# Attention of a hybrid diffusion step in units of 512 queries: plain float32 value products on two column halves

## The chip, the core and the metric

The kernel runs on one core of one Trainium2 chip. Its engines work side by side, each through its own queue in order: TensorE (PE, with its weight loads PEld), VectorE (DVE), ScalarE (ACT), GpSimd (POOL) and SyncE (SP, which issues DMAs). The metric is the device time of one execution in microseconds (us). The runs of the kernel before took 2245.47 to 2252.65 us, with a median of 2249.08 over three.

## The reference

One layer with 128 context tokens and 1024 latent tokens, all in float32. Its input projection feeds multi-head attention (8 heads) and an mLSTM; both are projected, gated and merged, and a feed-forward part follows. The part that the change touches is the attention of one block of queries:

```python
def block(args):
    qn_b, qp_b = args
    s = jnp.einsum('bqhd,bkhd->bhqk', qn_b, k_nope) + jnp.einsum('bqhr,bkr->bhqk', qp_b, k_pe)
    p = jax.nn.softmax(s.astype(jnp.float32) * MLA_SCALE, axis=-1)
    return jnp.einsum('bhqk,bkhv->bqhv', p.astype(v.dtype), v)
```

A query has 64 + 32 = 96 features per head, a value 64. Latent queries read 1024 latent and 128 cached context keys, which is 9 blocks of 128 keys; the 128 queries of the new context read only their own 128 keys.

## The kernel before

Most products are made exact by splitting: an operand x becomes hi (x rounded to float32r, `R32`) and lo (the rest), by `hi` on ACT (L69) and `lo` on DVE (L75). `mm3` (L98 to L100) then adds three float32r products hi*hi, hi*lo, lo*hi. Products of plain float32 (`F32`) operands are one instruction in the program, which leaves two records in the trace.

`attention` goes through the heads. For each head the 1024 latent queries are cut into four units of 256, and there is a small unit (`None`) for the 128 context queries. A unit's work, in program order:

- `maxima`: for each 128 queries three products of the leading parts against 384 keys (tile `mx`), a maximum on DVE for each (`sm`, then `mr`), and one product per 128 queries with a selector `sel` that turns the maxima into a row of the queries' operand. This is done for the unit ahead while the present one is scored.
- `scores`: five slots of two key blocks; each slot has two `mm3` into one bank `st`, the exponential on ACT (`p`), its split into `ph` and `pl` (DVE, in two slots of five POOL), and the running sum `es` on POOL.
- `values`: with a lag of two slots, four products of 256 columns per slot into `pv`. The stationary tile `v` holds 64 columns of hi and 64 of lo.
- `output`: the sum of `es` over its partitions by one-column products with `ones`, a reciprocal `rd` split into `rh` and `rl`, four diagonal matrices `dr` on ACT, two products that broadcast them, then a copy, an addition and a multiplication (`av`), a split (`ao`) and a store to `d_att`.

Beside this runs `o_mlstm`, the projection of the mLSTM's branch (tiles `hm` and `mm`, 384 columns): a share of its pieces is emitted in every slot. At the end `first` emits products of the attention's own projection (288 columns, tile `att`), which don't need the last heads' outputs; the tiles of the last pair of heads are reloaded from `d_att` by POOL's queue (`aload`).

The order in each engine's queue is not the program order: a scheduler in the build (`schedule_with_timeline_sim=True`) places ready instructions of later steps ahead. The queues then run in that fixed order.

Of the kernel before, what the change touches and what calls it, by code (L numbers as in the profile page):

```python
# [19 lines left out]
P = 128  # L20
# [36 lines left out]
class K:  # L57
# [25 lines left out]
    def load_w(self, src, kt, w, bufs=None):  # L83
        """Stream one weight block [P, kt, w] from DRAM and split it exactly."""
# [10 lines left out]
    def mm3(self, out, lhs, rhs, first, last):  # L95
        """out += lhs.T @ rhs for operands split in two parts."""
        mm = self.nc.tensor.matmul
        mm(out, lhs[0], rhs[0], start=first, stop=False)  # L98
        mm(out, lhs[0], rhs[1], start=False, stop=False)  # L99
        self.pe = mm(out, lhs[1], rhs[0], start=False, stop=last).ins  # L100
# [11 lines left out]
    def rsqrt(self, ssq, width, n, pool):  # L112
        """1/sqrt(ssq/n + eps) on the vector engine: exponent estimate and three Newton steps."""
# [12 lines left out]
    def row_rstd(self, rbc, acc, n, pool, pp, tag, chunks=CHUNKS, more=None):  # L126
        """rbc[:, t] = 1/sqrt(sum_p (acc[p, t] + more[p, t])/n + eps) on every partition."""
# [30 lines left out]
    def modulate(self, raw, t, sc, sh, k):  # L158
        """raw = t * sc + sh with the context's and the sample's own columns."""
# [4 lines left out]
    # ------------------------------------------------------------------  # L164
# [74 lines left out]
    def tick(self, n=1):  # L239
        """Emit n pieces of the work that runs beside the products."""  # L240
# [18 lines left out]
    def rows(self, rbc, acc, n, pool, pp, tag):  # L259
        """rbc[:, t] = 1/sqrt(sum_p acc[p, t]/n + eps) on every partition."""  # L260
# [28 lines left out]
    def inputs(self):  # L289
        """Everything that reads the modulated input (all of w_in), the mLSTM and the attention's projections."""  # L290
# [38 lines left out]
    def start(self, vp):  # L329
        """Norm and modulation of the input, and the mLSTM's values."""  # L330
# [44 lines left out]
        def row(f):  # L375
            """Shift (f even) or scale of block 6 + f // 2 of the features, as rows against the broadcast condition."""
# [166 lines left out]
    def t_ops(self, X, xp):  # L543
        """The four sums on the moving side."""
# [29 lines left out]
    def z_lat(self, x):  # L574
        """Latents and their norms, and the tile with gates and rotary key."""
# [40 lines left out]
    def z_qk(self, h, x):  # L616
        """q and k of one mLSTM head, S^T and k^T."""
# [29 lines left out]
    def z_big(self, p, x):  # L647
        """sigmoid(zmo) * g_mlstm for tiles 0-7, the sigmoids of the branch gates after them."""
# [17 lines left out]
    def background(self):  # L666
        """Columns of the modulation that are used after the mixer, as rows against the broadcast condition."""
# [41 lines left out]
    def krope(self):  # L709
        """Rotary keys, 288 tokens to a row."""  # L710
# [85 lines left out]
        # N = -M, A = log of the denominator's floor  # L796
# [24 lines left out]
    def lat_kv(self):  # L821
        """The key and value latent, back from DRAM and split."""
# [19 lines left out]
    def stage(self):  # L842
        """Half a slot for a projected block."""
# [11 lines left out]
    def proj(self):  # L855
        """Keys, values and queries of the attention from the latents."""
# [94 lines left out]
    def fill(self, n=1):  # L951
        """Emit n column chunks of the attention's projections."""
# [5 lines left out]
    # ------------------------------------------------------------------  # L958
    FILL = (17, 1, 1, 0, 1)

    def z2(self, mm):
# [4 lines left out]
        self.ready = False  # L966
        head = None
# [71 lines left out]
    def mfront(self, d, c, carried, second, S, E, Q, W):  # L1039
        """Operands of one chunk of one direction, four heads."""  # L1040
# [20 lines left out]
    def mback(self, d, c, carried, second, A, Q, K, C, mp, pp, side, load):  # L1061
        """Products, state update and output of the chunk."""
# [46 lines left out]
    def mpost(self, c, out, ssq, sgs, mp, pp):  # L1109
        """Norm, output gate and transposition of a finished chunk."""  # L1110
# [22 lines left out]
    # ------------------------------------------------------------------  # L1133
    def operands(self, pool):
        """Queries, keys and values of one head in two parts; row 96 adds -max of a query to its scores."""
        q = pool.tile([QK + 1, 2, T], R32, name=self.nm("q"))
        k = pool.tile([QK + 1, 2, NK], R32, name=self.nm("k"))
        v = pool.tile([P, NCH + 1, P], R32, name=self.nm("v"))
# [4 lines left out]
    def head_load(self, h, pool=None):  # L1143
        """Queries, keys (context, latent, cache) and values of one head, as column blocks."""
        G = self.nc.sync
        v = self.wp.tile([P, NCH + 1, AV], F32, name=self.nm("rv"), tag="wr", bufs=self.wb[0])
# [18 lines left out]
        G.dma_start(v, self.d_vo[h])  # L1165
        return q, k, v

    def head_split(self, h, raw):
        q, k, v = self.sets[h % 2]
        rq, rk, rv = raw  # L1170
# [5 lines left out]
        self.hi(v[:, :, 0:AV], rv)  # L1176
        self.lo(v[:, :, AV:], rv, v[:, :, 0:AV])
        yield 1

    SLOTS = 5  # L1180
    LAG = 2

    def attention(self):
# [6 lines left out]
        with tc.tile_pool(name="at", bufs=1, reuse_waits="tile") as ap:  # L1190
            self.ap, self.pp = ap, pp
            first = lambda shape, tag, bufs, dt=R32: ap.tile(shape, dt, name=self.nm(tag), tag=tag, bufs=bufs)
            for tag in ("ph", "pl"):
                first([P, 2, 256], tag, 4)
            first([P, 2, 256], "es", 2, F32)
            first([P, 2, 2, P], "dr", 1)
            first([AV, 256], "av", 2, F32)
            first([AV, 2, 256], "ao", 2)
            self.sets.append(self.operands(ap))
            self.onr = ap.tile([P, AV], R32, name="onr")  # L1200
            self.hi(self.onr, self.ones[:, 0:AV])
            self.sel = ap.tile([P, 3 * P], R32, name="selr")
            for i, x in enumerate((0.0, 1.0, 0.0)):
                self.hi(self.sel[:, i * P:(i + 1) * P], self.ident, x)
# [847 lines left out]
```

## Time and profile before

| | |
|---|---|
| runs, us | 2249.08, 2252.65, 2245.47 |
| profiled execution | span 2242.8 us from the first to the last instruction; its time with what lies around the span is not recorded |
| granted TensorE clock, mean | 0.966 |
| attention, first maxima to last division | 848 to 1263 us |

The profile shows one execution. Busy shares are of the span. A matmul's record reaches from its start to its modelled end, and records overlap, so the work of TensorE is better read from the distance between two starts. "Idle before" names what ended an engine's wait. The granted clock is the share of full speed that TensorE was given.

### The profile page before, as it was taken

The page shows a single profiled execution, that of the slowest core. Times are in us where ns is not written, and L with a number is a line of the kernel's source. Part 1 is how long each engine was busy: PE and PEld are TensorE (multiplying, and loading weights), DVE is VectorE, ACT ScalarE, POOL GpSimd, SP SyncE. Part 2 cuts the span into 40 slices and gives each one's busy share as a digit, 9 for nine tenths or more (in the row PEclk, how much of TensorE's full clock was granted, in tenths as well). Part 3 has the DMA queues.
Part 4 walks back from the last instruction along what each step waited for, and adds up shares of the span by engine and source line. Part 5 has one row for each costly group of instructions (what it writes and reads, how often), then busy time and mean ns, then how long its engine had stood idle before and what let it go on. Part 6 is the DMA issues. An engine that isn't in the chain of part 4 may idle for free.

```text
span 2242.8 us, 40186 instructions
## 1 busy us (share of the span) xinstructions
PE 2083.1 (93%) x14713; PEld 1998.2 (89%) x14713; DVE 1659.5 (74%) x2998; ACT 1068.0 (48%) x2225; POOL 1127.2 (50%) x850
## 2 busy tenths in 40 slices
PE   6799999999989987999999999879999999989898
PEld 2799998999978776998998999879999999989897
DVE  6725745988845879998987666899755565799895
ACT  4322333445445556777776435444322222356464
POOL 3612122667624415877877543677867634431411
PEclk8899999999999998999999999999999999999899
DMA  7121244555479775322224575223555522557664
GB/s 286 63 93 59 90 142 124 164 174 183 152 241 330 238 230 175 90 74 65 84 66 102 170 224 157 86 83 122 186 177 183 175 89 80 161 173 248 206 201 138
DMA packets 234532, 340.97 MB, mean 152 GB/s; under 512 B 18110, under 2 KB 170398, under 8 KB 233310
## 3 DMA queue, kind: packets, MB, share of 16 engines
q1 hardware_dynamic: 225790, 328.73, 46.0%
q0 software_dynamic: 4848, 6.06, 1.1%
q10 hardware_dynamic: 3696, 3.61, 0.5%
q8 instruction: 116, 1.90, 0.4%
q14 instruction: 82, 0.67, 0.1%
HBM read 250.55 MB, written 87.80 MB: 151 GB/s over the span
## 4 chain that ended last, share of the span: by engine, by line
PE 42%; DVE 16%; DMA 7%; POOL 6%; issue 6%; ACT 2%; SPq 1%; DVEq 0%; POOLq 0%; ACTq 0%
PE mm L98 10%; PE mm L100 10%; PE mm L99 10%; DVE wo L75 4%; DMA pr<-w_fo 3%; DVE sm L1374 2%; DVE pl L75 1%; PE st L98 1%; PE pv L1437 1%; PE pv L1438 1%; PE st L100 1%; PE st L99 1%; PE mx L1372 1%; DMA N<-d_nm 1%; PE p L1079 1%
## 5 line engine op out<-in xcount | busy, mean ns | idle before, releaser
L100 PE MATMUL mm<-th,wo 128*128 128x288 f32 x1840 | 546.8, 298 | 14.0 <-DVE wo L75 13.7
L98 PE MATMUL mm<-th,wo 128*128 128x288 f32 x1840 | 547.6, 298 | 2.7 <-DVE zo L1658 1.1
L99 PE MATMUL mm<-tl,wo 128*128 128x288 f32 x1840 | 546.2, 297 | 0.0
L100 PEld LDWEIGHTS mm<-th,wo 128*128 128x128 f32 x1840 | 348.9, 190 | 18.2 <-DVE wo L75 17.6
L75 DVE TENSOR_TENSOR wo<-wr,wo 128x512 fp32r<-128x512 f32 (+1 forms) x317 | 314.6, 1008 | 59.4 <-ACT wo L69 54.4
L98 PEld LDWEIGHTS mm<-th,wo 128*128 128x128 f32 x1840 | 348.2, 189 | 4.5 <-issue 1.6
L99 PEld LDWEIGHTS mm<-tl,wo 128*128 128x128 f32 x1840 | 348.3, 189 | 0.1
L69 ACT ACTIVATE wo<-wr 128x512 fp32r<-128x512 f32 (+1 forms) x317 | 187.5, 607 | 147.9 <-PE mm L100 69.5
L69 ACT ACTIVATE wo<-ws 128x512 fp32r<-128x512 f32 x188 | 116.7, 627 | 271.7 <-PE mm L100 160.5
L75 DVE TENSOR_TENSOR wo<-ws,wo 128x512 fp32r<-128x512 f32 x188 | 186.7, 996 | 62.1 <-ACT wo L69 61.9
L100 PE MATMUL mm<-xh,wo 128*128 128x288 f32 x616 | 184.7, 301 | 10.3 <-DVE wo L75 10.3
L1642 POOL TENSOR_TENSOR ws<-wr,ws 128x512 f32<-128x512 f32 x47 | 62.3, 1326 | 243.5 <-DVE wo L75 238.2
L99 PE MATMUL mm<-xl,wo 128*128 128x288 f32 x616 | 184.7, 300 | 0.0
L98 PE MATMUL mm<-xh,wo 128*128 128x288 f32 x616 | 184.2, 299 | 0.5 <-ACT wo L69 0.5
L1420 POOL TENSOR_TENSOR es<-es,p 128x512 f32<-128x512 f32 (+1 forms) x96 | 129.4, 1348 | 34.8 <-ACT p L1403 19.9
L98 PE MATMUL mm<-B,wo 128*128 128x288 f32 x456 | 134.8, 296 | 2.6 <-DVE zo L1658 1.7
L100 PE MATMUL mm<-B,wo 128*128 128x288 f32 x456 | 134.8, 296 | 0.0
L99 PE MATMUL mm<-B,wo 128*128 128x288 f32 x456 | 134.8, 296 | 0.0
L701 POOL TENSOR_TENSOR wm<-wm,sr 128x512 f32<-128x512 f32 x64 | 100.1, 1567 | 65.2 <-DVE mj L700 49.2
L100 PEld LDWEIGHTS mm<-xh,wo 128*128 128x128 f32 x616 | 118.1, 192 | 12.7 <-DVE wo L75 12.5
L98 PEld LDWEIGHTS mm<-xh,wo 128*128 128x128 f32 x616 | 118.2, 192 | 0.7 <-ACT wo L69 0.7
L99 PEld LDWEIGHTS mm<-xl,wo 128*128 128x128 f32 x616 | 118.4, 192 | 0.0
(443 smaller groups left out, 6076.6 us busy)
## 6 DMA issues: line engine op xcount, KB each, us to landing
wr<-w_ff SPq DMA_DIRECT2D x56, 512.0 KB
wm<-wm SPq DMA_DIRECT2D x32, 512.0 KB
wr<-d_w SPq DMA_DIRECT2D x32, 512.0 KB
d_z<-zo SPq DMA_DIRECT2D x48, 288.0 KB
d_g<-uu SPq DMA_DIRECT2D x44, 288.0 KB
wr<-w_big SPq DMA_DIRECT2D x24, 512.0 KB
wr<-w_fo SPq DMA_DIRECT2D x24, 512.0 KB
pr<-w_fo SPq DMA_DIRECT2D x40, 256.0 KB
```

Of the source, the lines that this page charges most:

```text
L69: i = self.nc.scalar.activation(out, in_, AF.Copy)
L75: return self.nc.vector.tensor_sub(out, in_, f32v(hi)).ins
L98: mm(out, lhs[0], rhs[0], start=first, stop=False)
L99: mm(out, lhs[0], rhs[1], start=False, stop=False)
L100: self.pe = mm(out, lhs[1], rhs[0], start=False, stop=last).ins
L701: nc.gpsimd.tensor_tensor(w[:, n], w[:, n], sr[:, 1], op=ALU.mult)
L1079: self.pe = mm(p1, A[:, h], V[:, h], start=True, stop=not carried).ins
L1372: nc.tensor.matmul(s[:, :kc], q[0:QK, 0, q0 + t * P:q0 + (t + 1) * P], k[0:QK, 0, k0 + j * kc:k0 + (j + 1) * kc], start=True, stop=True)
L1374: nc.vector.tensor_reduce(sm[:, 3 * t + j:3 * t + j + 1], s[:, :kc], axis=AX.X, op=ALU.max, negate=True)
L1420: G.tensor_tensor(U["sum"][:, :m], U["sum"][:, :m], p[:, :m], op=ALU.add)
L1437: nc.tensor.matmul(pv[:, :n], v[:, i], ph[:, e, :n], start=c + e == 0, stop=False)
L1642: G.tensor_tensor(s4, a12, s2, op=ALU.subtract)
```

## The change

- A unit has 512 queries (`QN`), so a head has two latent units and the small one. A slot of `scores` is one key block with 512 queries, nine slots to a unit.
- The exponentials `p` stay plain float32 and are not split; neither are the values, whose tile `v` has 64 columns and is filled by a DMA after the splits of the next head's queries and keys.
- `values` waits until a batch of a unit's blocks is ready (blocks 0 to 3, then 4 to 8) and emits plain float32 products of 64 stationary columns: even blocks into partitions 0 to 63 of `pv`, odd ones into 64 to 127, and the ninth block with half of its queries in each.
- `output` broadcasts the sum with two products of `ones` (64 columns) on the two halves, takes the reciprocal of 256 columns, adds the two halves and multiplies. The diagonal matrices and the selector are gone.
- `maxima` of all units are one stream, which runs up to two units ahead; the row of 512 maxima is written by four products of 128 columns with the identity.
- `o_mlstm` is spread over 136 - 11 slots in place of 168 - 13, so it ends earlier relative to the units.

```diff
-            units = [(h, b) for h in range(HA) for b in ((0, 1, 2, 3, None) if h < HA - 1 else (None, 0, 1, 2, 3))]
+            units = [(h, b) for h in range(HA) for b in ((0, None, 1) if h < HA - 1 else (None, 0, 1))]
...
-            NS, N0, NOM = HA * (4 * self.SLOTS + 1), 13, 88
+            NS, N0, NOM = HA * (2 * NCH - 1), 11, 88
...
-        p = self.wp.tile([P, 2, 256], F32, name=self.nm("p"), tag="ws", bufs=3)
-        self.ia = nc.scalar.activation(p[:, :m, :n], st[:, :m, :n], AF.Exp).ins
-        ph, pl = (ap.tile([P, 2, 256], R32, name=self.nm(x), tag=x, bufs=4) for x in ("ph", "pl"))
-        self.hi(ph[:, :m, :n], p[:, :m, :n])
...
+        self.mm3(st[:, :n], (k[:, 0, ks], k[:, 1, ks]), (q[:, 0, qs], q[:, 1, qs]), True, True)
+        p = U["P"][c] = ap.tile([P, self.QN], F32, name=self.nm("p"), tag="p", bufs=self.PBUF)
+        self.ia = nc.scalar.activation(p[:, :n], st[:, :n], AF.Exp).ins
...
-            nc.tensor.matmul(pv[:, :n], v[:, i], ph[:, e, :n], start=c + e == 0, stop=False)
-            self.pe = nc.tensor.matmul(pv[:, :n], v[:, i], pl[:, e, :n], start=False, stop=i == kb[-1]).ins
...
+            if len(todo) > 1:
+                parts = [(todo.pop(0), 0, n) for _ in range(2)]
+            else:
+                c = todo.pop(0)
+                parts = [(c, t * n // 2, n // 2) for t in range(2)]
+            for g, (c, q0, w) in enumerate(parts):
+                self.pe = nc.tensor.matmul(pv[g * AV:(g + 1) * AV, q0:q0 + w], v[:, kb[c]], U["P"][c][:, q0:q0 + w], start=c < 2,
+                                           stop=c == U["nc"] - 1, skip_group_check=True).ins
...
-        for t in range(nt):
-            nc.tensor.matmul(pv[:, 256 + t:257 + t], U["sum"][:, 0, t * P:(t + 1) * P], self.ones[:, 0:1], start=True, stop=True)
...
+        bc = self.bank(self.pp, "pv")
+        for g in range(2):
+            nc.tensor.matmul(bc[g * AV:(g + 1) * AV, :m], self.ones[:, 0:AV], U["sum"][:, g * m:(g + 1) * m], start=True, stop=True,
+                             skip_group_check=True)
```

TensorE's queue amid the latent units of one head. `pv` is the accumulator, `st` the scores, `mx` the maxima, `mm` the mLSTM's projection; the shape is that of the output. Before, the value products of two slots stand together, four to a slot:

```order
L1372 MATMUL mx_12035<-k_6950,q_6949 128x384
L1437 MATMUL pv_11792<-ph_11726,v_9240 128x256
L1438 MATMUL pv_11792<-pl_11727,v_9240 128x256
L1437 MATMUL pv_11792<-ph_11726,v_9240 128x256
L1438 MATMUL pv_11792<-pl_11727,v_9240 128x256
L1437 MATMUL pv_11792<-ph_11751,v_9240 128x256
L1438 MATMUL pv_11792<-pl_11752,v_9240 128x256
L98 MATMUL mm_11684<-hm_9497,wh_11191 128x384
```

All of them use the full 128 columns, like their neighbours. In the changed kernel, within one unit:

```order
L100 MATMUL mm_10610<-hm_9430,wl_10340 128x384
L1439 MATMUL pv_10690<-p_10623,v_9235 64x512
L1373 MATMUL mx_10630<-k_9234,q_9233 128x384
L1373 MATMUL mx_10646<-k_9234,q_9233 128x384
L98 MATMUL st_10677<-q_9233,k_9234 128x512
L99 MATMUL st_10677<-q_9233,k_9234 128x512
L100 MATMUL st_10677<-q_9233,k_9234 128x512
L1439 MATMUL pv_10690<-p_10643,v_9235 64x512
L1439 MATMUL pv_10690<-p_10662,v_9235 64x512
L98 MATMUL st_10697<-q_9233,k_9234 128x512
```

The scheduler has taken the batch apart: a 64-column product of one half stands alone between 128-column products, and a pair follows later.

At the unit's end, after the change, the ninth block and the broadcast of the sum stand together behind one product of 512 columns:

```order
L100 MATMUL st_10774<-q_9233,k_9234 128x128
L1439 MATMUL pv_10690<-p_10755,v_9235 64x512
L1439 MATMUL pv_10690<-p_10770,v_9235 64x256 x2
L1452 MATMUL pv_10794<-es_10625,ones 64x256 x2
L98 MATMUL mm_10742<-hm_9309,wh_10738 128x384
```

Before, the one-column products of the sum (L1449) and the two broadcasts (L1462) stood apart, with other products between them.

Behind the last division of the stage the queue before goes on with the mLSTM's projection, 110 products ahead of the first that reads the reloaded tile; its beginning:

```order
L1462 MATMUL pv_14795<-dr_14881,onr 64x256
L98 MATMUL pv_15028<-att_14408,wo_14965 128x288
L99 MATMUL pv_15028<-att_14408,wo_14965 128x288
L98 MATMUL mm_14929<-hm_9308,wh_14720 128x384
L99 MATMUL mm_14929<-hm_9308,wh_14720 128x384
```

Those 24 products of 384 columns are gone from this place. After, 45 products of 288 columns stand there; the last of them and the first reader of the reloaded tile (`att_12761`):

```order
L98 MATMUL st_12861<-rq_2349_12574,wo_12854 128x288
L99 MATMUL st_12861<-rq_2349_12574,wo_12854 128x288
L100 MATMUL st_12861<-rq_2349_12574,wo_12854 128x288
L98 MATMUL mx_12678<-att_12761,wo_12644 128x288
L99 MATMUL mx_12678<-att_12761,wo_12644 128x288
```

So the reader stands 45 rows behind the last division, where 110 stood before.

More of the change, by code (lines that the diff above doesn't have):

```diff
@@ L1192, in attention @@
             first = lambda shape, tag, bufs, dt=R32: ap.tile(shape, dt, name=self.nm(tag), tag=tag, bufs=bufs)
[L1193 to L1198, printed above, removed]
-            self.sets.append(self.operands(ap))
[L1200 to L1204, printed above, removed]
+            first([P, self.QN], "p", self.PBUF, F32)
+            first([P, self.QN], "es", 2, F32)
+            first([P, self.QN // 2], "av", 2, F32)
+            first([P, 2, self.QN // 2], "ao", 2)
+            self.sets.append(self.operands(ap))
+            self.idr = ap.tile([P, P], R32, name="idr")
+            self.hi(self.idr, self.ident)
             for tag in ("mm", "pv", "st", "mx"):
@@ L1210, in attention, with ahead @@
             side = []
-            units = [(h, b) for h in range(HA) for b in ((0, 1, 2, 3, None) if h < HA - 1 else (None, 0, 1, 2, 3))]
-            for _ in self.maxima(*units[0]):
-                pass
+            units = [(h, b) for h in range(HA) for b in ((0, None, 1) if h < HA - 1 else (None, 0, 1))]
+            mx = [self.maxima(*u) for u in units]
+            at = 0
+            def ahead(i, n=1):
+                nonlocal at
+                while n and at <= min(i, len(units) - 1) and units[at][0] in self.split:
+                    if next(mx[at], None) is None:
+                        at += 1
+                    else:
+                        n -= 1
@@ L1255, in attention @@
                                 next(self.om, None)
[L1256 to L1259 removed]
+            while late:
+                self.values(late)
             self.ps = {}
@@ L1427, in values, with ripe @@
+    def ripe(self, late, n):
+        U = late[0][1]
+        last = U["batch"][0][-1]
+        return any(t <= n and u is U and c == last for t, u, c in late)
+    def values(self, late):
+        nc = self.nc
+        U = late[0][1]
+        b = U["batch"].pop(0)
+        del late[:len(b)]
         h, n, kb = U["h"], U["n"], U["kb"]
         v = self.sets[h % 2][2]
-        if c == 0:
+        if b[0] == 0:
             while len(self.post) > 1:
```

182 lines of the change are left out of this document (81 added, 101 removed).

## The prediction

> **What bounds the kernel now.** I read the page's busy shares first, then the windows around attention, then the groups of instructions there, the waits, and single rows of the timeline.
>
> ```profile
> PE 2083.1 (93%) x14713; PEld 1998.2 (89%) x14713; DVE 1659.5 (74%) x2998; ACT 1068.0 (48%) x2225; POOL 1127.2 (50%) x850
> ```
>
> TensorE is busy 93% of the span, so time spent on it anywhere reaches the end. All edited lines run in the attention stage, from the first maxima at 848 us to the last division at 1263 us:
>
> ```profile
> core 0: us, PE busy (x) PEld busy (x) DVE busy (x) ACT busy (x) POOL busy (x), PEclk, DMA share, GB/s
> 848.00:900.00 52.00, 40.27 (x218) 34.11 (x217) 49.33 (x79) 36.16 (x72) 34.11 (x25) 0.80 0.53 161
> 900.00:1250.00 350.00, 331.83 (x2284) 314.57 (x2283) 307.16 (x611) 251.19 (x578) 262.92 (x212) 0.97 0.29 80
> 1250.00:1263.00 13.00, 12.28 (x86) 12.01 (x85) 5.42 (x9) 3.66 (x11) 5.38 (x6) 1.00 0.28 79
> ```
>
> The columns are length, then busy time of PE, weight loads, DVE, ACT, POOL, then granted clock. The first 52 us are bound by DVE (49.3 busy) and run at a clock of 0.80. After that PE is busy 95% and DVE 88%: two engines near their limit.
>
> PE's busy times overlap, so its work must be counted by distances between starts:
>
> ```profile
> 1060.49 0.28 PE L98 MATMUL st<-q,k 97*128 97x256 f32 x1
> ...
> 1061.91 0.28 PE L1382 MATMUL mx<-selr,mr 128*1 128x256 f32 x1
> 1062.21 0.22 PE L1462 MATMUL pv<-dr,onr 128*64 128x128 f32 x1
> 1062.27 0.39 PE L1372 MATMUL mx<-k,q 96*128 96x384 f32 x1
> 1255.07 0.34 PE L98 MATMUL mm<-hm,wh 128*128 128x384 f32 x1
> ...
> 1255.60 0.33 PE L98 MATMUL mm<-hm,wh 128*128 128x384 f32 x1
> 30.70 0.56 PE L267 MATMUL mm<-ones,ar 128*128 128x1 f32 x4
> 31.18 3.60 PE L356 MATMUL mx<-wm,silc 128*2 128x512 f32 x8
> 34.71 0.27 PE L267 MATMUL mm<-ones,ar 128*128 128x1 f32 x1
> 28.58 1.02 PE L356 MATMUL mx<-wm,silc 128*2 128x512 f32 x2
> 29.53 0.38 PE L280 MATMUL mm<-dg,ones 128*128 128x128 f32 x1
> 1500.62 0.40 PE L100 MATMUL mm<-th,wo 128*128 128x288 f32 x1 [1.08 <-DVE wo L75]
> 1500.86 0.30 PE L98 MATMUL mm<-th,wo 128*128 128x288 f32 x1
> ```
>
> In split (fp32r) products, 256 columns take 0.118 us (twelve products from 1060.49 to 1061.91), 128 take 0.06 and 384 take 0.177. The plain float32 product L356 leaves two records per product; eight last 3.60 with the last 0.59 of it, so (3.60 - 0.59)/7 = 0.430 a record and 0.86 for 512 columns. Half a record is 0.215, the stream of 512 columns, so a split product of 512 takes 0.215 + 0.0105 = 0.2255 (the 0.0105 is what 0.118 holds beyond 0.1075). A float32 product of one column has records at about 0.10 (0.56 less the 0.27 of one, over three). The 288-column products of the tail stand 0.133 apart.
>
> **The change part by part**, in us of PE time.
>
> ```profile
> L98 PE MATMUL st<-q,k 97*128 97x256 f32 x288 | 86.1, 299 | 1.5 <-ACT p L1403 0.9 <-ACT q L1383 0.4
> L1437 PE MATMUL pv<-ph,v 128*128 128x256 f32 x288 | 81.8, 299 | 5.7 <-DVE av L1467 5.7
> L1372 PE MATMUL mx<-k,q 96*128 96x384 f32 x192 | 65.2, 375 | 10.6 <-DVE sm L1374 9.8
> L1382 PE MATMUL mx<-selr,mr 128*1 128x256 f32 x72 | 20.0, 289 | 8.3 <-DVE mr L1377 4.0 <-DVE mr L1379 3.7 <-DVE sm L1374 0.4
> L1462 PE MATMUL pv<-dr,onr 128*64 128x256 f32 x64 | 17.7, 284 | 0.1
> L1449 PE MATMUL pv<-ones,es 128*128 128x1 f32 x128 | 16.3, 230 | 0.3 <-POOL es L1422 0.3
> ```
>
> Scores: 3 x 288 products of 256 columns (102.0) become 432 of 512 (97.4): -4.6. The maxima stay at 192 products. Their row transposes go from 72 x 0.118 to 72 of 128 columns at 0.06: -3.9 with rounding to 0.064.
>
> Values and division before: 576 x 0.118 = 68.0, the context's 16 at 0.06 = 1.0, 144 one-column records x 0.10 = 14.4, broadcasts 64 x 0.118 + 16 x 0.06 = 8.5; together 91.9. After, end to end: 128 products of 512 columns x 0.86 = 110.1, 64 of 256 x 0.43 = 27.5, 32 of 64 columns at about 0.12 = 3.8; together 141.5. Two halves can overlap only where products of different halves stand next to each other in PE's queue. In the built order the 224 products stand in 134 separate runs, 78 of them one single product of 512 columns; there are 90 neighbours of different halves. A product's two records use the same half, so each pair of neighbours overlaps by one record: 21 x 0.43 + 49 x 0.215 + 20 small = 20.6. Net 141.5 - 20.6 - 91.9 = +29.0. Whether halves overlap at all no row shows; the bounds are none (+49.6) and full halving to 70.8 (-21.1). I take the overlap only where partners stand, as in the order.
>
> Going between 64-column and 128-column products: L356 has two stationary columns, its neighbours 128. L267 starts at 34.71, which is 8 x 0.430 + 0.09 after 31.18; L280 at 29.53, where 28.58 + 0.86 gives 29.44: again 0.09. The first product behind also lasts longer since its weights could not be loaded ahead; the restart at 1500.62 shows that price, 0.40 against 0.30. For 64 columns I take half of it:
>
> ```profile
> L1462 PEld LDWEIGHTS pv<-dr,onr 128*64 128x64 f32 x80 | 11.0, 138 | 2.2 <-ACT dr L1459 1.2 <-issue 0.2
> L356 PEld LDWEIGHTS mx<-wm,silc 128*2 128x2 f32 x48 | 4.3, 95 | 31.4 <-issue 19.1 <-ACT silc L393 6.4 <-DMA wm<-wm 5.9
> ```
>
> since 62 more columns cost 0.138 - 0.095 = 0.043. One run then costs 0.09 + 0.05 going in and 0.09 + 0.10 coming out, 0.33; 134 runs cost +44.2. Bounds: 0 if the 0.09 belongs to L356 alone and the loads hide, 51 if both loads are full ones.
>
> A rule speaks against the change here. L356's weight load is hidden, for its records follow at the bare stream of 0.430. The Trainium skill, TensorE: Matmul & The Clock Gate, Part 3 (The mechanism), says that a weight load overlaps running products only when the row group differs; column halves share their rows. By it each of the 448 records would show its load of 0.05, an estimate of +22 on the sum; the 0.430 of the same tile speaks against it, and I take nothing.
>
> What the other engines shed:
>
> ```profile
> L75 DVE TENSOR_TENSOR pl<-p,ph 128x512 fp32r<-128x512 f32 x96 | 88.5, 924 | 20.9 <-ACT ph L69 18.7 <-issue 1.9
> L75 DVE TENSOR_TENSOR rl<-rd,rh 128x2 f32<-128x2 f32 x32 | 22.1, 691 | 0.3
> L1374 DVE TENSOR_REDUCE sm<-mx 128x1 f32<-128x384 f32 x192 | 99.7, 543 | 9.9 <-PE mx L1372 9.3
> L69 ACT ACTIVATE ph<-p 128x512 fp32r<-128x512 f32 x128 | 79.0, 626 | 3.5 <-PE pv L1437 1.3 <-PE pv L1438 1.0
> L1466 DVE TENSOR_TENSOR av<-av,pv 64x256 f32<-64x256 f32 x31 | 12.5, 402 | 0.2 <-ACT av L1465 0.2
> L1451 DVE RECIPROCAL rd<-pv 128x2 f32<-128x2 f32 x32 | 5.0, 157 | 3.8 <-PE pv L1449 3.8
> ```
>
> DVE loses 110 of 362 us (pl and rl) and gains 16 reciprocals over 256 columns, without a row: between 0.4 each (an addition over 256) and 20 (0.157 for two columns, times 128). A reciprocal that slow would show at each unit's end; I take about 0.5, 8 in all, since the other elementwise rows of 256 lie there. ACT loses 79 and more. POOL keeps 128 sums and loses 64 subtractions. None of them is near its limit any more, so these gains count only through PE's lost time.
>
> That lost time: PE's counted work is 341 (102.0 + 91.9 + 8.5, scores of the context 1.4, maxima 33.9, 552 products hm x 0.174 = 96, 51 tail products x 0.133 = 6.8) in 415 us, so 74 are lost: 30.6 idle by the windows, 52 x 0.20 + 350 x 0.03 = 21 by the clock, the rest restarts. Nearly all named waits are DVE's:
>
> ```profile
> PE mx L1372 <- DVE sm L1374: 10.0, 13, 2.0
> PE pv L1437 <- DVE av L1467: 5.7, 5, 2.5
> PE mx L1382 <- DVE mr L1377: 4.0, 6, 1.0
> ```
>
> I take 40 of the 74 as saved; bounds 0 and 60. The early stage keeps its splits of hm and the maxima on DVE and now needs twelve maxima before the first score.
>
> The end: the last division is covered less.
>
> ```profile
> 1262.74 0.28 PE L1462 MATMUL pv<-dr,onr 128*64 128x256 f32 x1
> 1265.25 0.52 SPq L1472 DMA_DIRECT2D d_att<-ao  x1
> 1270.54 1.45 POOL L1312 DMA_DIRECT2D att<-d_att  x2
> att<-d_att POOLq DMA_DIRECT2D x14, 288.0 KB, 6.6
> ```
>
> From the last division to the landing of the reload are 1270.54 + 6.6 - 1262.74 = 14.4. Before, 110 products (24 hm, 86 of 288) stand behind it ahead of the first use: 24 x 0.174 + 86 x 0.133 = 15.6. After, the hm products are used up earlier and 45 of 288 stand there: 6.0. So +9 (bounds 0 and 10); late next is the reload on POOL's queue. On SP's queue the values' load goes behind the splits and waits for the values of two heads before; stores and hm's loads behind it wait too, by less than a unit's slack, taken as 0 (0 to 5).
>
> Sum: -4.6 - 3.9 + 29.0 + 44.2 - 40 + 9 = +34. Against this execution's span of 2242.8 that gives 2277; what lies around the span is not shown, and the median of the runs, 2249.1, is 6.3 above it. I predict 2283 us.
>
> **The rivals.** (1) Faster: going between the two widths costs nothing, so the 44.2 is gone: 34 - 44 = -10, 2239. The sign turns where a run costs under 34/134 = 0.25 us. For it: the gap is seen on a two-column product only. Against: it is the same 0.09 in both places. (2) Halves never overlap: +20.6, 2304. (3) The lost time is not DVE's and stays: +40, 2323; against it stand the waits above. (4) The lost time nearly vanishes (60): 2263. (5) The values halve fully, neighbours or not: 34 - (141.5 - 20.6 - 70.8) = -16, 2233; the 78 single runs speak against it. The Trainium skill, TensorEngine Tiling (Array Packing), Theoretical Speedup, gives up to 2x at 64 columns or fewer, which is this case; no run here shows it yet.
>
> **How the numbers follow.** My forecast has 0.50, (1) 0.15, (2) 0.13, (3) 0.10, (4) 0.07, (5) 0.05. Its own range, by the bounds of the lost time and the switch, is 2255 to 2305. The range 2236 to 2325 takes in all but (5) and the far ends. Faster by over 0.3% (7 us, about what a measurement of this kernel can tell from none) are (1) and (5), 0.20; 0.05 lies between, from (4) and the forecast's low end; slower 0.75.
>
> **What would show it.** Right: value products about 1.2 us apart from the split products around them when single, with gaps of 0.09 to 0.2 on either side; neighbours starting one record apart; DVE under 65% from 900 on; PE's waits for DVE under 10 us; a wait for the reload after the last division. Wrong: single value products with no gap around them, or a PE row that waits on ACT or POOL throughout the stage.

## The result and the profile after

The changed kernel took 2271.91 us (median; 2266.25 to 2272.58), the kernel before 2247.28 us beside it: a ratio of 1.0108, with a 95% interval of 1.008 to 1.0136. It is slower, by 24.6 us; 34 were forecast. The profiled execution has a span of 2270.8 us, 28.0 more than before.

The page's busy shares of the changed kernel, and its windows over the same stretches (columns as before):

```profile
PE 2124.3 (94%) x13913; PEld 1904.9 (84%) x13913; DVE 1531.7 (67%) x2710; ACT 927.7 (41%) x1846; POOL 1009.1 (44%) x754
848.00:900.00 52.00, 44.92 (x143) 23.20 (x142) 38.21 (x62) 25.41 (x44) 21.46 (x16) 0.80 0.58 172
900.00:1250.00 350.00, 342.02 (x1507) 217.89 (x1507) 186.04 (x340) 118.07 (x224) 148.82 (x117) 0.99 0.28 76
```

Everything but TensorE has become lighter: between 900 and 1250 us VectorE went from 307 to 186 us (53%), ScalarE from 251 to 118, GpSimd from 263 to 149. TensorE's busy time went up, from 332 to 342 of 350. The change has taken work from engines that were not the bound and left more on the one that is.

Where TensorE's time goes stands in the timeline. First a single product of 512 columns (L1439) between products of 128 columns, then a pair of different halves; `x2` and `x4` are records, two to a product:

```profile
1063.98 0.34 PE L99 MATMUL mm<-hm,wh 128*128 128x384 f32 x1
1064.16 0.34 PE L100 MATMUL mm<-hm,wl 128*128 128x384 f32 x1
1064.43 1.07 PE L1439 MATMUL pv<-p,v 128*64 128x512 f32 x2
1065.43 0.44 PE L1373 MATMUL mx<-k,q 96*128 96x384 f32 x1
1065.71 0.40 PE L98 MATMUL st<-q,k 97*128 97x512 f32 x1
...
866.42 0.39 PE L100 MATMUL st<-q,k 97*128 97x512 f32 x1
866.74 1.08 PE L1439 MATMUL pv<-p,v 128*64 128x512 f32 x4
867.75 0.50 PE L98 MATMUL st<-q,k 97*128 97x512 f32 x1
```

Read the distances between starts. Two products of 384 columns stand 0.18 apart (1063.98, 1064.16). From the second to the single value product it is 0.27, from there to the next 1.00, and that one takes 0.28: 1.55 in all. Without a change of width these three would take 0.177 + 0.86 + 0.177 = 1.21. So one single product costs 0.34 us for going into 64 columns and out again. The pair below goes in and out in the same 1.01 us, though it is two products: both records of one half ran beside both records of the other. The loads under that pair:

```profile
866.74 0.20 PEld L1439 LDWEIGHTS pv<-p,v 128*64 128x64 f32 x4 [0.36 <-issue]
867.75 0.19 PEld L98 LDWEIGHTS st<-q,k 97*128 97x128 f32 x1 [0.81 <-issue]
```

All four weight loads are done 0.20 us after the pair's start, below its stream of 0.86. The load of the next, wider product waited until 867.75. The rule of the Trainium skill that the prediction weighed (TensorE: Matmul & The Clock Gate, Part 3, The mechanism: a load overlaps running products only where the row group differs) does not hold for these column halves.

TensorE's waits in the stage, by engine and line waited for (us, times, longest):

```profile
PE mx L1384 <- DVE mr L1378: 5.3, 3, 2.9
PE st L98 <- DVE fl L1525: 3.5, 1, 3.5
PE mx L98 <- DMA att<-d_att: 1.9, 1, 1.9
...
PE mx L1373 <- DVE sm L1375: 0.6, 1, 0.6
```

The wait for the maxima fell from 10.0 to 0.6 us, while at the end the wait for the merge's first bank grew from 1.0 to 3.5 and the wait for the reload is new.

**Where the 28.0 us lie.** First maxima to last division went from 414.7 to 437.7 us (847.90 to 1285.56). In that stretch now stand 24 products of 384 columns and 24 of 288 that came behind the last division before; that is 7.4 us of moved work, so attention itself costs 15.6 more. Counted from the end of the program to the same product, the piece from the last division to the end of the reload lost another 8.6. Some 4 us more arise at 1698 to 1759 us, in the feed-forward part, where nothing was edited (a wait of 2.8 us, and a granted clock of 0.94 there); they are of this execution, and the medians, 24.6 apart, do not have them.

### The profile page after: what moved, and what is told of

Read it like the earlier page. It is cut to its first block, busy times and chain, and to the rows that moved or that the text cites. A ratio compares the mean times of both kernels' runs of the same rounds, so it can differ in the third digit from the quotient of the medians.

```text
span 2270.8 us, 37661 instructions
## 1 busy us (share of the span) xinstructions
PE 2124.3 (94%) x13913; PEld 1904.9 (84%) x13913; DVE 1531.7 (67%) x2710; ACT 927.7 (41%) x1846; POOL 1009.1 (44%) x754
## 4 chain that ended last, share of the span: by engine, by line
PE 53%; DVE 10%; DMA 6%; POOL 5%; issue 4%; ACT 2%; SPq 1%; DVEq 0%; ACTq 0%; POOLq 0%
PE mm L98 12%; PE mm L100 12%; PE mm L99 12%; PE pv L1439 5%; DVE wo L75 4%; DMA pr<-w_fo 2%; PE st L98 2%; PE mx L1373 2%; PE st L100 2%; PE st L99 2%; PE p L1080 1%; POOL wm L701 1%; DMA S<-d_s 1%; PE p L1082 1%; POOL ps L1733 0%
## 5 line engine op out<-in xcount | busy, mean ns | idle before, releaser
L1409 POOL TENSOR_TENSOR es<-es,p 128x512 f32<-128x512 f32 x112 | 152.6, 1363 | 122.1 <-ACT p L1402 118.9
L1375 DVE TENSOR_REDUCE sm<-mx 128x1 f32<-128x384 f32 (+1 forms) x200 | 102.3, 539 | 151.4 <-PE mx L1373 150.9
L1402 ACT ACTIVATE p<-st 128x512 f32<-128x512 f32 (+1 forms) x152 | 87.9, 580 | 191.9 <-PE st L100 182.8
L1439 PE MATMUL pv<-p,v 128*64 128x512 f32 (+2 forms) x352 | 128.0, 548 | 1.5 <-DVE av L1464 1.5
```

Source lines behind the costliest of these rows:

```text
L1375: self.iv = nc.vector.tensor_reduce(sm[:, t, j:j + 1], s[:, :kc], axis=AX.X, op=ALU.max, negate=True).ins
L1402: self.ia = nc.scalar.activation(p[:, :n], st[:, :n], AF.Exp).ins
L1409: nc.gpsimd.tensor_tensor(U["sum"], U["sum"], p, op=ALU.add)
L1439: self.pe = nc.tensor.matmul(pv[g * AV:(g + 1) * AV, q0:q0 + w], v[:, kb[c]], U["P"][c][:, q0:q0 + w], start=c < 2, stop=c == U["nc"] - 1, ...
```

## Experiments

Medians are compared with the changed kernel's 2271.91 and with the kernel before, run beside each; its median on the chips used lay between 2244.9 and 2248.2 us. A stage's time is the distance from the first maxima to one fixed product of the merge behind the reload, 459.3 us in the changed kernel, so that work moved across the last division does not show. Lines of these kernels can be up to five higher than those of the changed one. Each has one profile, of a single execution, which can lie some microseconds from its median.

### Batches held together

```diff
+        self.sc = self.pe                      # in scores, behind its mm3
...
+                with self.tc.issue_after(self.sc):
                     self.pe = nc.tensor.matmul(pv[g * AV:(g + 1) * AV, q0:q0 + w], ...
```

> The value products of a batch may not be placed ahead of the scores that precede them in the program, so they become ready together: 80 separate runs of 64-column products in TensorE's queue in place of 134, 14 single products in place of 78. Theory S (each run costs 0.33 us for going between the widths, and neighbours of different halves overlap in both records, as the changed kernel's trace shows): 54 x 0.33 = 18 us from the switches and about 27 us from the products that now find a partner, 45 in all, so about 2227 us. Rival O (the halves' overlap counts, but the switches are hidden by other losses): -27, 2245 us. Rival W (the products held back leave TensorE waiting for exponentials or sums, which eats the gain): 2260 to 2275 us, with new named waits before the scores.

Measured: 2239.19 us, ratio to before 0.9973 (0.9961 to 0.9986): 33 us below the changed kernel and 0.3% below the kernel before. The stage fell by 30.6 us, to 428.7. Four value products in one run, from the timeline:

```profile
924.70 0.40 PE L100 MATMUL st<-q,k 97*128 97x512 f32 x1
925.02 1.94 PE L1441 MATMUL pv<-p,v 128*64 128x512 f32 x8
926.89 0.50 PE L98 MATMUL st<-q,k 97*128 97x512 f32 x1
```

Four products take 1.87 us from start to next start, 2 x 0.86 and 0.15: the stream of two. Counted run by run at these distances, the values' streams shrank by 27 us (109 to 82), as theory S had it, and 54 runs less give 18.4. That is some 45 of gain, of which 30.6 arrived; 7 of the rest went into waits, which rose from 21 to 28 us in the stage:

```profile
PE mx L1384 <- DVE mr L1378: 8.9, 3, 5.5
PE st L98 <- ACT q L1385: 5.0, 10, 1.0
```

About 3 us more are value products that fell into stretches of half clock; the last 4 to 5 are not located. Theory S is right in kind, and W takes a part of it. O is out: with nothing for the switches, 27 us of overlap less 7 of new waits would leave 20.

### One half first

```diff
-                parts = [(todo.pop(0), 0, n) for _ in range(2)]
...
-            for g, (c, q0, w) in enumerate(parts):
+                parts += [(g, todo.pop(0), 0, n) for g in range(2)]
...
+        for g, c, q0, w in sorted(parts, key=lambda x: x[0]):
```

> As e1_together, but within a batch all products of one half come first, then those of the other (A A B B in place of A B A B); 78 runs. If TensorE takes the records in the order of its queue (theory of the prediction: neighbours overlap by one record only), only one record per batch overlaps: about 40 us above e1_together. If the two halves run independently of each other in any order: at most 10 us above e1_together.

Measured: 2253.15 us (ratio to before 1.004, 1.0023 to 1.0057), 14 us above the kernel with A B A B: far below the 40 of queue order, though above the 10 that were set for halves in any order. Its timeline, at two batches:

```profile
1245.42 1.94 PE L1441 MATMUL pv<-p,v 128*64 128x512 f32 x8
1247.30 0.44 PE L98 MATMUL mm<-hm,wh 128*128 128x384 f32 x1
...
960.03 3.28 PE L1441 MATMUL pv<-p,v 128*64 128x512 f32 x12
963.24 0.50 PE L98 MATMUL st<-q,k 97*128 97x512 f32 x1
```

A A B B takes 1.88 us, as A B A B did: the first B starts 0.013 us behind the first A although four records of A stand ahead of it. So the halves do not run in the order of the queue, and the prediction's picture (a neighbour overlaps by one record) is wrong. But the batch of five, with three products of A and then three of B, takes 3.21 in place of 2.30: there the first B starts 0.915 us late, with A's third record. A half can run ahead of the other past four records, not past six. Nine such batches give 8 of the 11 us by which the stage is longer than in the first experiment. A finer count of that depth was not tried.

### Values at full width

```diff
-                self.pe = nc.tensor.matmul(pv[g * AV:(g + 1) * AV, q0:q0 + w], v[:, kb[c]], ..., start=c < 2,
+                self.pe = nc.tensor.matmul(pv[:, q0:q0 + w], v[:, kb[c]:kb[c] + 2], ..., start=c < 1,
```

> As the changed kernel, but each value product has 128 stationary columns: the 64 of its own key block and 64 of the next one (the sums of the second 64 are not used and the two accumulations fall together, so the output is not the attention's). No product of the values is narrower than its neighbours then, and none can overlap another half; the broadcasts keep 64 columns in 24 runs. Theory S: 110 runs x 0.33 = -36 us of switching, +41 us of lost overlap, so about 2275 us, and in the trace the single value products show no 0.09 us gap. Rival F (the 0.33 us belongs to going between float32r and plain float32, not to the width): the gaps stay, +41 us, about 2312 us.

Measured: 2258.15 us, 13.8 below the changed kernel; the stage lost 14.6. Single products in its timeline:

```profile
1106.76 0.39 PE L100 MATMUL st<-q,k 97*128 97x512 f32 x1
1106.99 1.02 PE L1440 MATMUL pv<-p,v 128*128 128x512 f32 x2
1107.45 0.74 PE L1374 MATMUL mx<-k,q 96*128 96x384 f32 x1
1108.02 1.02 PE L1440 MATMUL pv<-p,v 128*128 128x512 f32 x2
```

The gap in is gone (0.23 from a product of 512, its own stream), and from one value product to the next, with a product of 384 between them, it is 1.03 = 0.86 + 0.17: the bare streams. So plain float32 alone does not make the 0.34; rival F is out. The width alone does not make it either. The kernel before has 64-column products of float32r (L1462, the broadcast) between products of 128 columns:

```profile
1262.62 0.29 PE L100 MATMUL pv<-att,wo 128*128 128x288 f32 x1
1262.74 0.28 PE L1462 MATMUL pv<-dr,onr 128*64 128x256 f32 x1
1262.86 0.29 PE L98 MATMUL pv<-att,wo 128*128 128x288 f32 x1
1262.99 0.30 PE L99 MATMUL pv<-att,wo 128*128 128x288 f32 x1
```

These stand 0.12, 0.12 and 0.13 us apart, which are the bare streams (0.133 for 288 columns, 0.118 for 256), with no gap on either side. So the 0.34 belongs to plain float32 products with 64 stationary columns among products with 128; what it is in that combination that costs time, no run shows. The expected total was 17 us too high: its 41 us of lost overlap count the sums' pairs too, which keep theirs. With the sums left as they are, the streams go from 109.8 to 133.7, +23.9, and 110 runs x 0.34 give -37.4: -13.5, which is what came.

### The splits put back

```diff
+        if n == self.QN:
+            ph = ap.tile([P, self.QN], R32, name=self.nm("ph"), tag="ph", bufs=2)
+            self.hi(ph, p)
+            if c % 3 < 2:
+                self.lo(ph, p, ph)
```

> As the changed kernel, with the splitting of the exponentials put back as work without use: 144 activations of 128x512 on ScalarE and 96 subtractions of 128x512 on VectorE, as many as before the change. 142 runs in the queue, so +3 us by them. Theory D (TensorE's lost time fell from 74 to about 46 us because VectorE and ScalarE were relieved): +15 to +30 us, 2290 to 2300 us, with waits for VectorE back. Rival N (the lost time was never VectorE's): +3 us, 2275 us.

Measured: 2284.46 us, +12.6; the stage +10.8. The edit also gives the output tile `ao` one buffer in place of two. The window shows VectorE with 253 us, and TensorE hardly touched; one wait at 880 us, in the early stage, is long:

```profile
900.00:1250.00 350.00, 340.73 (x1461) 212.25 (x1459) 253.05 (x408) 179.64 (x334) 148.88 (x113) 0.98 0.27 73
...
PE pv L1444 <- DVE rd L1464: 4.5, 1, 4.5
```

TensorE is busy 340.7 of 350, 342.0 without that load. Of the 10.8 us the queue's 8 more runs give 2.7 and the values' streams, with fewer partners, 4.5; some 3.6 are left. TensorE's waits in the stage rose only from 21.0 to 21.6 us in all; the one of 4.5 us for VectorE's reciprocal, in the early stage, stands in place of one of 1.5. So by the trace VectorE had room for this work: nearer to rival N than to theory D, whose range begins at 15. The total alone does not decide it: by the ratios to the kernel before (1.0185 against 1.0108) the distance is 17 us, and the profiled execution, of 2276.32 us, is the fastest of the four. The expectation's 46 us of lost time are 31 in the count further down.

### The kernel before without the low parts

```diff
-            self.iv = self.lo(pl[:, :m, :n], p[:, :m, :n], ph[:, :m, :n])
+            pl = ph
```

> The kernel before, but VectorE's 96 subtractions of 128x512 (88.5 us) that make the low parts of the exponentials are left out; the leading parts are multiplied twice in their place, so TensorE's products are as many and as wide as before, and the attention's output is wrong. Theory D (the prediction: TensorE's lost time of 74 us is VectorE's; 40 us of it go when VectorE is relieved): -25 to -40 us, 2207 to 2222 us. Theory B (that relief is not what took TensorE's idle time from 30.6 to 15.1 us; half as many unit ends and a queue with longer products did): 0 to -10 us, 2237 to 2247 us.

Measured: 2222.61 us, ratio 0.9894 (0.9867 to 0.9921), by which it is 24 us faster, just short of theory D's range and far outside theory B's. The edit also moves the point behind which the scheduler places other work (`self.iv`) from the subtraction to the maxima, so the queues' order is not quite that of before. Its window and its waits, to be held against those of before:

```profile
900.00:1250.00 350.00, 342.78 (x2413) 331.12 (x2412) 240.63 (x527) 257.31 (x591) 239.15 (x219) 0.98 0.31 84
...
PE mx L1372 <- DVE sm L1374: 4.2, 9, 1.3
PE mx L1382 <- DVE mr L1377: 2.1, 5, 0.8
```

With VectorE at 241 of 350 us in place of 307, TensorE's idle time between 848 and 1250 us fell from 29.9 to 16.0, in the changed kernel to 15.1. There VectorE was the second bound, as the prediction read it. Both results fit together: busy 88% between 900 and 1250 us, VectorE holds TensorE up; busy 72% (the run above), hardly. How much of the saving in the changed kernel is the relief, and how much that there are half as many unit ends, is between these two, 3.6 and 24, and not settled further.

### Maxima one unit ahead

```diff
-                    ahead(i + 2, 2)
+                    ahead(i + 1, 2)
```

> As the changed kernel, but the stream of maxima may run only one unit ahead of the unit being scored, as before the change, not two. 141 runs in the queue (+7 x 0.34 = 2.4 us). Theory M (TensorE's idle time in the stage fell from 30.6 to 15.1 us since the maxima are ready in time, not since VectorE and ScalarE split less): waits for VectorE's maxima come back, +8 to +15 us, 2280 to 2290 us. Rival R (idle time fell because there are half as many unit boundaries, whatever the lead): within 4 us of the changed kernel, 2274 us.

Measured: 2277.24 us, +5.3, between the two ranges (3 us by the ratios to the kernel before); the stage +4.5, of which 2.4 are the seven runs more. The wait that theory M called for did not come:

```profile
PE mx L1384 <- DVE mr L1378: 5.1, 4, 2.9
PE mx L1373 <- DVE sm L1375: 0.6, 1, 0.6
```

Both are what they were (5.3 and 0.6). The second unit of lead is worth at most some 3 us.

### The end covered

```diff
-            NS, N0, NOM = HA * (2 * NCH - 1), 11, 88
+            NS, N0, NOM = HA * (2 * NCH - 1) + 14, 11, 88
```

> As the changed kernel, with the mLSTM's projection spread over 150 - 11 slots in place of 136 - 11, so that part of it is left for the end: behind the last division 39 products of 384 columns (6.8 us) are back in TensorE's queue ahead of the reload's readers. The queue has 145 separate runs of value products in place of 134. Theory T (8.6 us between the last division and the end of the reload are a wait that has lost its cover): the piece from the last division to the end of the reload falls by 6 to 8 us for the same work, while 11 x 0.34 = 4 us come on by the switches, so 2268 to 2270 us; the waits for the reload in the trace fall from 6.1 to under 2. Rival U (the wait comes from a load or an engine that the cover doesn't hide): the waits stay at 6, 2276 us.

Measured: 2264.49 us, -7.4, where theory T gave -2 to -4, though the queue has 11 more runs. In the profiles the stage fell by 13.5, but from there to the end it is 5.0 us longer (968.6 in place of 963.6), and why is open. Behind the last division only one wait has a name:

```profile
PE mx L100 <- DVE wo L75: 0.8, 1, 0.8
```

The end's loss, its time less its products at their streams, fell from 10.0 to 0.8 us, which is theory T's 6 to 8 and a little more; ahead of the last division TensorE's waits fell too, from 16 to 11 us, which neither theory had. What the changed kernel shows there, in its timeline and in windows:

```profile
1293.99 0.40 PE L98 MATMUL st<-att,wo 128*128 128x288 f32 x1 [3.46 <-DVE fl L1525]
1298.73 0.61 PE L98 MATMUL mx<-att,wo 128*128 128x288 f32 x1 [1.89 <-DMA att<-d_att]
...
1294.00:1296.40 2.40, 2.40 (x12) 2.40 (x12) 0.52 (x2) 0.45 (x1) 1.44 (x2) 0.60 1.01 288
1296.40:1298.70 2.30, 0.44 (x2) 0.09 (x1) 1.33 (x4) 0.73 (x2) 1.34 (x3) 0.50 1.18 365
1298.70:1304.60 5.90, 5.87 (x24) 5.87 (x25) 2.76 (x7) 1.23 (x4) 2.64 (x4) 0.50 1.00 366
1304.70:1310.00 5.30, 5.30 (x41) 5.30 (x41) 5.09 (x9) 3.37 (x8) 2.69 (x4) 1.00 0.41 117
```

The waits are only part of the loss. After the first of them the clock column goes to 0.60 and 0.50 until 1304.6: the products of 288 columns then stand 0.24 apart in place of 0.133. Here a wait is paid twice. The first wait also shows a chain that the prediction did not have: on SP's queue the loads of `fl` (1290.42 us) stand behind the store of the last division (1289.14), and the merge's first bank waits for them.

### Closer still

Three kernels went on from the first experiment. The first emits the values three blocks behind the scores and covers the end, the second covers the end and emits the broadcast of the sums a block later, the third does all of this.

```diff
-    LAG = 2
+    LAG = 3                                        # first and third
...
-            NS, N0, NOM = HA * (2 * NCH - 1), 11, 88
+            NS, N0, NOM = HA * (2 * NCH - 1) + 20, 11, 88
...
+        yield 1                                    # in output, second and third
         bc = self.bank(self.pp, "pv")
         for g in range(2):
+          with self.tc.issue_after(self.sc):
```

> As e1_together, with the values emitted three blocks behind the scores in place of two, and the mLSTM's projection spread over 156 - 11 slots: 68 separate runs (80), 5 single products (14), and 27 products of 384 columns behind the last division. Against e1_together, theory S gives 12 x 0.34 = 4 us from the switches and about 9 x 0.6 = 5 us from the products that find a partner, theory T 5 us from the cover: 14 in all, about 2226 us. Rival W (what e1_together gave back, waits for the maxima's row at the units' starts, grows as the products stand closer): 2239 us or more.

> e1_together with the cover of the end (the mLSTM's projection over 156 - 11 slots) and with the broadcast of the sums emitted one block later, not ahead of the scores of that block: 70 runs (80), 8 broadcasts standing in one run with the values ahead of them. Against e1_together (2239 us): 10 x 0.34 = 3 us from the switches, 7 us from the cover (its end lost 7.7 us), so about 2229 us. Rival W (waits for sums and maxima's rows take it back, as in e7): 2238 us or more.

> As e7 (values three blocks behind the scores, the cover), with the broadcast of the sums one block later: 53 runs in place of 68. e7 waited 10.0 us for the sums on GpSimd at the broadcasts. If that wait is only a matter of place, it falls under 3 us and the switches give 15 x 0.34 = 5 us: 2248 - 12 = 2236 us. If GpSimd's sums (1.3 us a block) bind now that the values stand together: 2245 us or more, with the wait for the sums still there.

Measured: 2247.99 us (ratio to before 1.0, 0.9983 to 1.0017), 2236.77 (0.9957, 0.9944 to 0.9971) and 2248.68 (1.0015, 0.9997 to 1.0033). The second is the fastest of those that leave nothing out, 35 us below the changed kernel and 0.4% below the kernel before, though not clearly below the first experiment; the stage went from 428.7 to 419.2 us in the profiles, but these are of an execution 5.6 us above the first experiment's median and one 4.1 below the second kernel's, so most of that is not the change. The other two have the fewest runs, 68 and 53, and the shortest streams of values, 7 and 10 us less than the first experiment at full clock, and are slower than it: TensorE's idle time in the stage, 28 us there, is 39 and 49 here. Their longest waits, of the first, then of the third (whose profile is of an execution 8 us above its median):

```profile
PE pv L1454 <- POOL es L1410: 10.0, 8, 2.6
PE mx L1384 <- DVE mr L1378: 9.8, 6, 4.0
...
PE mm L98 <- DVE t L1355: 14.0, 5, 4.4
PE mx L1384 <- DVE mr L1378: 12.7, 6, 3.5
```

So neither expectation for the third came true: emitting the sums later took away the wait for GpSimd (10.0 us), and others took its place. TensorE now waits in pieces of up to 4.4 us for VectorE, which is at the splits of the next head and the maxima. One such piece of the third kernel in windows:

```profile
1080.50:1084.60 4.10, 0.02 (x1) 0.03 (x1) 4.10 (x8) 0.08 (x1) 1.42 (x1) 0.92 0.33 99
1084.60:1086.00 1.40, 1.40 (x4) 1.40 (x5) 0.00 (x0) 0.00 (x0) 0.00 (x0) 0.50 0.69 199
1086.00:1090.00 4.00, 4.00 (x15) 2.64 (x16) 1.06 (x3) 0.87 (x2) 0.00 (x0) 0.50 0.46 134
1090.00:1095.00 5.00, 5.00 (x17) 1.77 (x18) 0.67 (x2) 0.87 (x3) 0.00 (x0) 0.58 0.07 27
1095.00:1098.00 3.00, 3.00 (x16) 2.73 (x16) 2.96 (x5) 0.76 (x2) 0.29 (x1) 1.00 0.00 0
```

VectorE works through all 4.1 us of the wait, TensorE comes back at half clock, and it is full again only ten microseconds later.

### The reciprocal

```diff
-        nc.vector.reciprocal(rd[:, :m], bc[:, :m])
+        nc.vector.tensor_copy(rd[:, :m], bc[:, :m])
```

The group of the reciprocals in the changed kernel, both shapes together:

```profile
L1459 DVE RECIPROCAL rd<-pv 128x256 f32<-128x256 f32 (+1 forms) x24 | 32.5, 1355 | 13.2 <-PE pv L1452 12.9
```

> The changed kernel, but the reciprocal of the broadcast sums (VectorE, 128x256, measured at 1.76 us each, 16 times 28 us in all) is replaced by a copy of the same size, so that the output is multiplied instead of divided. 138 runs in the queue (134): +1.4 us. Theory H (the prediction took 0.5 us for a reciprocal; the 20 us more are hidden, since VectorE is busy 53% between 900 and 1250 us): within 4 us of the changed kernel, 2268 to 2276 us. Rival V (units' ends wait for it): -8 to -15 us, about 2260 us.

> The same replacement in e8_together_cover_sumlater, in which TensorE's work is shorter by some 40 us and VectorE's the same. Theory H: within 4 us of e8 (2237 us). Rival V: 2225 to 2230 us, with fewer waits for the maxima's rows, which stand behind the reciprocal on VectorE.

Measured: 2272.09 us, 0.2 above the changed kernel, and 2230.40 us (ratio 0.9944, 0.9924 to 0.9965) against 2236.77 (0.9957) of the kernel it was made from. In the changed kernel that is within theory H's 4 us, so the reciprocal is hidden but for a few microseconds. How few is open: the queue without it has 4 more runs and 88 single products in place of 78, some 6 us of TensorE's work, which a gain may have covered; and behind the last division, where the reciprocal stands ahead of the store, the piece to the same product is 1.2 us shorter (20.5 in place of 21.7). In the shorter kernel (73 runs in place of 70) the intervals overlap, so a gain of a few microseconds is possible and not shown.

## Why the prediction was right

By its own steps, in us, measured by distances between starts in the profiled execution; the lost time is what the 437.7 us hold beside 360.9 of counted work and 45.6 of switches:

| step | predicted | measured |
|---|---|---|
| scores | -4.6 | -1.3 (432 x 0.233) |
| transposes of the maxima | -3.9 | -4.2 (72 x 0.059) |
| values and sums, after overlap | +29.0 (120.9) | +17.9 (109.8) |
| going between the widths | +44.2 (134 x 0.33) | +45.6 (134 x 0.34) |
| TensorE's lost time in attention | -40 | -43 (74 to 31) |
| cover of the end | +9 | +8.6 |
| sum | +34 | +24, to the end of the reload |

- **The switch** was the term that decided the sign, and its sum held to a hundredth of a microsecond: 0.27 - 0.177 in, 1.00 - 0.86 and 0.28 - 0.177 out. That closeness is part luck. The prediction had 0.14 going in and 0.19 coming out; 0.09 and 0.24 came, and the two errors cancel. Both of its readings were of the way out of a product of two columns. And it ascribed the cost to the two widths. The full-width run shows that the narrow width is needed; a row that the prediction itself shows, a 64-column product of float32r with a bare 0.06 to the next start (1062.21 to 1062.27), shows that plain float32 is needed as well.
- The prediction's remark on rival (1), that the sign turns where a run costs under 34/134 = 0.25 us, is a slip. That is by how much a run would have to be cheaper; by its own terms the sign turns at (44.2 - 34)/134 = 0.08.
- **The overlap** is the mis-sized term, by 11 us: neighbours of different halves overlap in both records, not in one. 141.5 end to end became 109.8, a saving of 31.7 in place of 20.6. Rival (5), full halving, did not come since 78 products stood alone, as the prediction argued.
- **The scores** gained less: products of 512 columns stand 0.233 apart, not the 0.2255 worked out from those of 256.
- **The lost time** came out near its number, but the ground given covers only part of it. The kernel before loses 24 us less with VectorE's 88.5 us taken away, so the reading of VectorE as second bound was right; putting the load back into the changed kernel leaves only some 4 us to it, so other parts of the change had made room as well. That 43 came for 40 is therefore in part luck.
- **The reciprocal** was taken at about 0.5 us and took 1.757 for 256 columns. The 20 us of error cost at most a few, as the run without it shows.
- **The end**: 8.6 us, but half of it is not the wait itself; it is the half clock behind the wait, which the prediction did not have: the waits grew from 1.0 to 5.4 us, and some 35 products at half clock give 4. Its 14.4 less 6.0 of cover arrived at the right size by another composition.
- Of the signs given ahead, single products do stand about 1.2 us apart with their gaps (1.00 + 0.27), VectorE is under 65% (53), and there is a wait for the reload. "Neighbours starting one record apart" was wrong: they start 0.007 us apart. TensorE's waits for VectorE, which were to be under 10 us, fell from 26 to some 12 up to the last division.

The forecast of 2283 was 11 us above the measured 2272. The steps account for 10 too many, of which the span's 4 us elsewhere take back 4; and 6.3 had been added for the median above the span, which is 1.1 here.

## What to carry to other kernels

Count in the built order how often TensorE changes between plain float32 products of 64 stationary columns and products of 128, and price each run at the gaps of the trace, before counting what halves may save: here 134 runs cost more (45.6 us) than the halves gave (31.7), and one ordering edge that kept a batch together won it back. Work taken from an engine that is not the bound pays only as far as that engine makes the bound wait; and a TensorE wait of two or more microseconds should be priced with the half clock behind it.

## What was not expected of the hardware

- After most waits of TensorE of 2 to 4 us the granted clock was 0.50 to 0.60, for 3.4 to 13.7 us. The kernel before has one too:

```profile
1032.00:1034.40 2.40, 0.40 (x3) 0.14 (x2) 2.37 (x4) 1.78 (x6) 1.88 (x2) 0.99 0.00 0
1034.40:1038.00 3.60, 3.58 (x14) 3.31 (x15) 3.09 (x8) 2.21 (x6) 2.67 (x2) 0.53 0.00 0
```

  Here 2.0 idle microseconds of 2.4 were enough for a clock of 0.53. The Trainium skill, TensorE: Matmul & The Clock Gate, Part 1 (The HAM clock gate), gives an idle window of about 3.4 us for the fall to half rate; the fall agrees with these windows, the length is shorter here. It is no sure thing: in the first experiment a wait of 2.5 us at the end left the clock at 1.00, the next, of 2.7, brought it to 0.64.
- A product with 64 stationary columns costs its bare stream among products of 128 when it is float32r, and 0.34 us more when it is plain float32.
- Two column halves have orders of their own: a product of the second half started 0.013 us behind the first of the other half, past four records that stood ahead of it in the queue, but not past six.
- VectorE's reciprocal took 1.757 us for 256 columns and 0.553 for 64, some 6.3 ns a column, where an addition of 256 took 0.41.
